# Two-layer streaming encoder on one core: raw weights, operand loads and tile choice in the seven-product MLP

## The chip, the cores and the metric

The kernel runs on one core of one Trainium2 chip. The metric is the device time of one execution in microseconds (us). The core has five engines, each with a queue of its own: TensorE (PE; its weight loads are PEld), VectorE (DVE), ScalarE (ACT), GpSimd (POOL) and SyncE (SP). In this kernel all the large transfers are issued from SP's queue.

## The reference

One step of an encoder with two trunk layers over 1024 prompt tokens and 32 sample tokens (1056 columns in all, model width 1024). Layer 0 mixes with an mLSTM, layer 1 with banded attention; each is followed by a layer norm and an MLP, which is all that matters here:

```python
        x = layer_norm(ALPHA * x + (1 + g1) * y, p['ln_g'][l, 0], p['ln_b'][l, 0])
        u = x * (1 + sc2) + sh2
        f = jnp.square(jax.nn.relu(u @ p['w_up'][l])) @ p['w_down'][l]
        x = layer_norm(ALPHA * x + (1 + g2) * f, p['ln_g'][l, 1], p['ln_b'][l, 1])
```

`w_up` is 1024 x 4096, `w_down` 4096 x 1024, all in float32.

## The kernel before

Every float32 operand is split into a high and a low part (`split`: a cast on ScalarE at L89, a subtraction on VectorE at L90), and a product is three matmuls (high x high, high x low, low x high).

The MLP of layer 1 is `mlp7`. The 1056 columns are cut into four quarters of `QN` = 264, and two quarters make a pair `tp` (`L.pairs` = 1, 0). Where it can, a 2 x 2 block product is made from seven block products instead of eight (`PRODS`, products 0 to 6); these use sums and differences of blocks, called forms.

**Up part.** 16 blocks `pb` of 256 columns of `w_up`. Ten (6 to 15) are first made plainly for pair 1 (`up_tile`, `up_unit`'s work, L1341 to L1376), while `tforms` makes the forms of `u` in `TF`, `ext` and `exu`. Then come 22 jobs (block, pair), numbered `j`; the last ones are blocks 11, 14, 12, 15, 13 for pair 0. A job is a `Seven`, whose `product(i)` is twelve matmuls (L1300). The jobs overlap: products are ordered by `7 * j + 2 * i`, so that a job's later products alternate with the next job's first. Product 6 ends with `h_forms`: it squares `H` (three buffers), splits it into `HL` and `HM` (one buffer each) and stores them, for blocks below 14 as the seven operand forms to `hd` in DRAM (L1172, L1177), for blocks 14 and 15 plainly to `hpl` (L1167).

**Weights.** `forms` is a generator for one block's weights: its first step issues two raw loads (L1248, tiles `rdn_u`, `rdn_d`, from a ring of three raw tiles), the later ones make the split forms `wf_u`, `wf_d`. `prep(n)` takes the first step, `advance(n, i)` the others, called after product `i` of block `n`.

**Down part.** 20 units: five groups `g` of blocks (`GRP`: two blocks in group 0, three in the others, so `kg` = 2 or 3), and in each four units `m` of 256 output columns. A unit is the seven products over both pairs (L1406), with an addition into `ACX` behind each (L986). `ACX` lies over the tiles of `TF`, and `L.reload(m)` (L1932) brings a quarter of it back from DRAM. The operands of a group are 14 loads (`fill`, `Rooms.load`, L1117) from `hd` into rooms: a list of quarter tiles, each with `KG` = 4 rooms, in `ep` (4), the two `u2` tiles (16 each), four `f4` tiles (16, over the place of `H`, `HL` and `HM`) and a ring tile (4). A load takes `kg` rooms from the head of the list, in one transfer for each run of adjacent ones. A group's rooms come back one form at a time during its last unit. The loads of group 0 begin in the up part, ten of them, as far as there are rooms.

**End.** Blocks 14 and 15 are made plainly from `hs`, four tiles in the place of the four `f4` tiles, loaded from `hpl` (L1472), with the columns in four blocks, and each block is normed and stored.

The order on each engine's queue is not that of the text. The text gives the order of importance; a planner that reckons with its own times for every instruction fixes the order at build time, except on PE, where in the marked regions (`manual_schedule`) the order of the text holds within the region. SP issues its transfers in the planned order, and each waits there until its tile is free or its data is ready.

Of the kernel before, what the change touches and what calls it, by code (L numbers as in the profile page):

```python
# [75 lines left out]
def trunk_kernel(ctx: ExitStack, tc: tile.TileContext, a, o):  # L76
# [10 lines left out]
    def split(dst_h, dst_l, src, eng=None):  # L87

        nc.scalar.copy(dst_h, src)  # L89
        (eng or nc.vector).tensor_sub(dst_l, src, dst_h.bitcast(F32))  # L90
# [1001 lines left out]
    GRP = [(0, 2), (2, 3), (5, 3), (8, 3), (11, 3)]  # L1092
# [31 lines left out]
    def mlp7(L):  # L1124
# [15 lines left out]
        rooms = Rooms()  # L1140

        def up_w(pb):
            if pb not in wups:
                wups[pb] = up_weights(l, pb)
            return wups[pb]
# [6 lines left out]
        def h_tile(pb, tp):  # L1152
            return hhp.tile([P, 6, QN], F32, tag="H", name=f"H{l}_{pb}_{tp}", bufs=3)

        def h_place(pb, tp):
            g = [i for i, (p0, kg) in enumerate(GRP) if p0 <= pb][-1]
            return hd[g][tp][:, :, pb - GRP[g][0]].rearrange("f p l t -> p f (l t)")

        def h_forms(pb, tp, H):

            nc.scalar.activation(H[:, 0:4], H[:, 0:4], AF.Square)
            hl = hhp.tile([P, 4, 2, QN], F32R, tag="HL", name=f"HL{l}_{pb}_{tp}", bufs=1)
            if pb >= NW:
                split(hl[:, :, 0], hl[:, :, 1], H[:, 0:4])
                for f, q, i in ((0, 1, 0), (0, 0, 1), (1, 1, 2), (1, 0, 3)):
                    t0 = (2 * tp + q) * QN
                    nc.sync.dma_start(hpl[2 * (pb - NW) + f, :, :, t0:t0 + QN], hl[:, i].bitcast(F32))  # L1167
                return
            dst = h_place(pb, tp)
            nc.vector.tensor_sub(H[:, 4:6], H[:, 0:3:2], bass.AP(H.tensor, H[:, 1].offset, [H.ap[0], [-QN, 2], [1, QN]]))  # L1170
            split(hl[:, :, 0], hl[:, :, 1], H[:, 1:5])
            nc.sync.dma_start(dst[:, 0:4], hl.bitcast(F32).rearrange("p f l t -> p f (l t)"))  # L1172
            nc.vector.tensor_sub(H[:, 1], H[:, 2], H[:, 4])
            nc.vector.tensor_sub(H[:, 3], H[:, 3], H[:, 1])
            hm = hhp.tile([P, 3, 2, QN], F32R, tag="HM", name=f"HM{l}_{pb}_{tp}", bufs=1)
            split(hm[:, :, 0], hm[:, :, 1], H[:, 1:6:2])
            nc.sync.dma_start(dst[:, 4:7], hm.bitcast(F32).rearrange("p f l t -> p f (l t)"))  # L1177

        def up_tile(pb, f, q):

            tp = q // 2
            ps = up_mm(pb, f, q)
            if (pb, tp) not in hts:
                hts[pb, tp] = [h_tile(pb, tp), 0]
            H = hts[pb, tp][0]
            nc.scalar.activation(H[:, ((1, 0), (3, 2))[f][q % 2]], ps, AF.Relu)
            hts[pb, tp][1] += 1
            if hts[pb, tp][1] == 4:
                h_forms(pb, tp, hts.pop((pb, tp))[0])
            flow.tick(QN / 96)  # L1190
# [42 lines left out]
        def moving(f, tp, hl, k):  # L1233
            if f in (B11, B21, B22, T4):
                kap, q = {B11: (0, 0), B21: (1, 0), B22: (1, 1), T4: (0, 1)}[f]
                return L.u4(hl, tp, kap, q)[:, k]
            if f == T3:
                return exts[tp][:, hl, k]
            return TF[tp, int(f == T2)][hl][:, k]
# [43 lines left out]
        class Seven:  # L1283
# [2 lines left out]
            def __init__(self, pb, tp, ws):  # L1286
                self.pb, self.tp, self.ws, self.ps = pb, tp, ws, {}

            def product(self, i):
                w, f, b, _, _ = PRODS[i]  # L1290
                pb, tp = self.pb, self.tp
                if i == 0:
                    self.H = h_tile(pb, tp)
                first = b not in self.ps
                if first:
                    self.ps[b] = mm(f"up{l}_{pb}_{tp}_{b}")[:, :QN]
                p, H = self.ps[b], self.H
                for k in range(4):
                    for n_, (wl, xl) in enumerate(((0, 0), (0, 1), (1, 0))):
                        nc.tensor.matmul(p, self.ws[w][:, wl, k], moving(f, tp, xl, k), start=first and k + n_ == 0,  # L1300
                                         stop=k == 3 and n_ == 2, skip_group_check=not first)
                if i in (0, 2, 3):
                    nc.scalar.copy(H[:, {0: 4, 2: 5, 3: 2}[i]], p)
                elif i in (1, 4, 5):
                    o_, x = {1: (1, 4), 4: (2, 2), 5: (0, 5)}[i]
                    nc.vector.tensor_add(H[:, o_], p, H[:, x])
                    if i == 5:
                        nc.scalar.activation(H[:, 0:3], H[:, 0:3], AF.Relu)
                else:
                    nc.scalar.activation(H[:, 3], p, AF.Relu)  # L1310
                    h_forms(pb, tp, H)
                flow.tick(QN / 64)

        tp0, tp1 = L.pairs
# [10 lines left out]
        jobs = [(n, tp) for n, (pb, tps) in enumerate(seq) for tp in tps]  # L1325
# [3 lines left out]
        def prep(n):  # L1329
            if n < len(makers):  # L1330
                preps[n] = makers[n]()
                next(preps[n])

        def advance(n, i):

            if n + 1 in preps and i in (0, 1, 3, 5):
                got[n + 1] = next(preps[n + 1])
            if i == 3:
                prep(n + 2)
        TF = {}  # L1340
        for i in range(2):  # L1341
# [12 lines left out]
        for j, pb in enumerate(rest):  # L1354
            for f in range(2):
                for q in L.quarters[:2]:
                    up_tile(pb, f, q)
                if (j, f) == (0, 1):
                    L.ready(2)
                    for n, tp in enumerate(L.pairs):  # L1360
                        for i, t in enumerate(L.scratch(n)):
                            TF[tp, i] = t
                    exts[tp1] = ring.tile([P, 2, KG, QN], F32R, tag="wc", name=f"exu_{l}", bufs=6)
                    tfs = [tf, tforms(tp1, exts[tp1])]
                at = 2 * j + f - 2 * len(rest) + 14
                if at == 11:
                    prep(0)
                for n in {1: (1,), 2: (1,), 3: (1,), 4: (1,), 5: (1,), 6: (1,), 7: (0,), 8: (0,), 11: (0, 2),
                          12: (2,), 13: (2, 0)}.get(at, ()):
                    if n < 2:  # L1370
                        next(tfs[n], None)
                    else:
                        got[0] = next(preps[0])
            del wups[pb]
            if j + 2 < len(rest):
                up_w(rest[j + 2])  # L1376
        fx, nfx, f4s = {}, {}, []
# [3 lines left out]
        def fill(g, into, most=99):  # L1381

            kg = GRP[g][1]
            if g >= len(GRP) - 2:
                rooms.free.sort(key=lambda r: any(r[0] is t for t in f4s) == (g == len(GRP) - 1))
            while want and len(rooms.free) >= kg and most:
                most -= 1
                tp, f = want.pop(0)
                into[tp, f] = rooms.load(hd[g][tp][f], kg)

# [23 lines left out]

        prep(1)
        got[0] = next(preps[0])
        lone = max(j for j, (_, tp) in enumerate(jobs) if tp == tp0)
        sevens = {}
        with tc.manual_schedule(engines={mybir.EngineType.PE}):
            for _, j, i in sorted((7 * j + 2 * i, j, i) for j in range(len(jobs)) for i in range(7)):  # L1420
                n, tp = jobs[j]
                if i == 0:
                    sevens[j] = Seven(seq[n][0], tp, got[n])
                sevens[j].product(i)
                if tp == seq[n][1][-1]:
                    advance(n, i)
                if j == lone and i == 6:
                    rooms.add(ep.tile([P, KG, 2, QN], F32R, tag="e", name=f"fx_e{l}"))
                    for t in L.rooms(tp0):
                        rooms.add(t)  # L1430
                if j > lone + 1:
                    if i in (0, 2, 4):
                        fill(0, fx, 1)
                    elif i == 6 and j < lone + 4:
                        L.reload(j - lone - 2)
        L.reload(2)
        nu = len(seq)
        hh_cm.__exit__(None, None, None)
        f4_cm = tc.tile_pool(name=f"f4{l}", bufs=1, reuse_waits="tile")
        f4p = f4_cm.__enter__()  # L1440
        f4s += [f4p.tile([P, KG, 2, QN], F32R, tag=f"f4{i}", name=f"fx_4{i}_{l}") for i in range(4)]
        for t in f4s:
            rooms.add(t)
        for t in L.rooms(tp1):
            rooms.add(t)
        fill(0, fx)
        with tc.manual_schedule(engines={mybir.EngineType.PE}):
            for i, (g, m, phases) in enumerate(units):
# [16 lines left out]
                if m == 3:  # L1465
                    assert not want
                    fx, nfx = nfx, {}
# [70 lines left out]
    for gi, grp in enumerate(((0, 1, 2), (3,))):  # L1538
        ws = {pr: [wblock(f"q{pr}_{half}", wq, 512 * half, 256 * pr) for half in range(2)] for pr in grp}
        for ti, (t0, n) in enumerate(TBS):  # L1540
# [7 lines left out]
            for fc in [f for pr in grp for f in (2 * pr, 2 * pr + 1)]:  # L1548
                g, r = fc // 2, 2 * (fc % 2)
# [309 lines left out]
    for ti in rev:  # L1859
        t0, n = TBS[ti]  # L1860
# [138 lines left out]
```

## Time and profile before

| what | value |
|---|---|
| median of 3 runs | 2477.54 us (2477.21 to 2479.55) |
| the profiled execution | 2478.93 us |
| its span in the profile | 2477.2 us |
| mean granted PE clock | 0.986 |
| instructions | 42903 |
| bytes moved by DMA | 335.17 MB |
| jobs of the up part on PE (L1300) | 1855 to 2094 us |
| down part on PE (L1406) | 2088 to 2400 us |
| last plain part (`hs`) on PE | 2406 to 2440 us |

Times in the profile are from the start of the span. A line such as `2104.11 12.06 SPq L1117 ... x12` means: from 2104.11 us on, for 12.06 us, twelve instructions of line 1117 on SP's queue; the brackets behind a line give how long the engine stood idle before it and what ended that. A line of the list of waits gives who waited for whom, the total in us, how often, and the longest.

### The profile page before, as it was taken

What the parts mean: (1) busy time and instruction counts of PE and PEld (TensorE: products, weight loads), DVE (VectorE), ACT (ScalarE), POOL (GpSimd) and SP (SyncE); (2) the same over time, 40 slices, a digit from 0 to 9 for tenths busy, and PEclk for the clock granted to TensorE, in tenths of its full rate; (3) what the DMA queues carried; (4) which work ended last, traced back from release to release, by engine and by line L of the source; (5) the groups of instructions that cost most, each with busy time, mean ns of one, the idle gap of its engine ahead of it and who ended that gap; (6) DMA issues with size and microseconds to landing.
All of it is one profiled execution on the core that took longest, in us unless ns stands there. A gap on an engine that the chain in (4) does not pass through costs nothing.

```text
span 2477.2 us, 42903 instructions
## 1 busy us (share of the span) xinstructions
PE 2391.2 (97%) x16580; PEld 2300.1 (93%) x16580; DVE 1921.3 (78%) x4340; ACT 1090.5 (44%) x2264; POOL 167.9 (7%) x315
## 2 busy tenths in 40 slices
PE   7999999999999999999999999999999997899997
PEld 4999999999999999999999877899999997899997
DVE  4898999778678679676597667747998887777768
ACT  4644456382211211212266567744866775222212
POOL 0211100000000000000001144400000000000003
PEclk9999999999999999999999999999999998999999
DMA  8433223313224224224132310052576788856632
GB/s 297 122 110 101 81 89 122 115 35 119 77 91 137 81 87 139 76 91 142 44 101 81 92 36 2 18 147 63 191 263 214 256 299 309 319 205 234 238 117 71
DMA packets 251072, 335.17 MB, mean 135 GB/s; under 512 B 12776, under 2 KB 201596, under 8 KB 249844
## 3 DMA queue, kind: packets, MB, share of 16 engines
q1 hardware_dynamic: 250868, 332.42, 41.0%
q8 instruction: 131, 2.15, 0.3%
q14 instruction: 73, 0.60, 0.1%
HBM read 255.50 MB, written 79.24 MB: 135 GB/s over the span
## 4 chain that ended last, share of the span: by engine, by line
PE 79%; DVE 10%; ACT 2%; DMA 2%; issue 2%; POOL 0%; SPq 0%; DVEq 0%; ACTq 0%; POOLq 0%
PE dn L1406 11%; PE up L1300 8%; PE up L120 6%; PE up L118 6%; PE up L119 6%; PE dn L119 5%; PE dn L118 5%; PE dn L120 5%; PE pv L1739 3%; PE s L1682 2%; PE pt L1717 2%; PE op_a L118 1%; PE op_a L119 1%; PE op_a L120 1%; PE o L118 1%
## 5 line engine op out<-in xcount | busy, mean ns | idle before, releaser
L1406 PE MATMUL dn<-fx,wf_d 128*128 128x264 f32 x2016 | 254.9, 286 | 17.0 <-DMA fx<-hd 12.0
L1406 PEld LDWEIGHTS dn<-fx,wf_d 128*128 128x128 f32 x2016 | 250.0, 189 | 18.5 <-DMA fx<-hd 12.2
L119 PE MATMUL dn<-h,w_dn 128*128 128x384 f32 (+1 forms) x768 | 249.5, 325 | 0.0
L118 PE MATMUL up<-U,w_up 128*128 128x384 f32 (+1 forms) x768 | 249.2, 325 | 0.0
L119 PE MATMUL up<-U,w_up 128*128 128x384 f32 (+1 forms) x768 | 247.9, 323 | 0.0
L118 PE MATMUL dn<-h,w_dn 128*128 128x384 f32 (+1 forms) x768 | 247.8, 323 | 0.0
L120 PE MATMUL up<-U,w_up 128*128 128x384 f32 (+1 forms) x768 | 247.6, 322 | 0.0
L120 PE MATMUL dn<-h,w_dn 128*128 128x384 f32 (+1 forms) x768 | 247.3, 322 | 0.0
L986 DVE SCALAR_TENSOR_TENSOR ACX<-dn,ada,ACX 128x264 f32<-128x264 f32 (+5 forms) x400 | 160.1, 427 | 66.7 <-PE dn L1406 47.5
L238 DVE SCALAR_TENSOR_TENSOR aacc<-rada,cs,aacc 128x256 f32<-128x256 f32 x448 | 190.4, 478 | 0.0
L986 DVE SCALAR_TENSOR_TENSOR acc<-dn,ada,acc 128x384 f32<-128x384 f32 (+2 forms) x256 | 119.4, 487 | 47.7 <-PE dn L120 46.4
L1025 ACT ACTIVATE r<-up 128x384 f32<-128x384 f32 (+1 forms) x96 | 44.3, 463 | 243.9 <-PE up L120 236.5
L1300 PE MATMUL up<-u,wf_u 128*128 128x264 f32 x1056 | 140.9, 286 | 8.5 <-ACT wf_u L89 8.0
L119 PEld LDWEIGHTS dn<-h,w_dn 128*128 128x128 f32 x768 | 144.5, 188 | 0.2 <-DVE h L1028 0.2
L120 PEld LDWEIGHTS dn<-h,w_dn 128*128 128x128 f32 x768 | 144.5, 188 | 0.0
L120 PEld LDWEIGHTS up<-U,w_up 128*128 128x128 f32 x768 | 144.3, 188 | 0.0
L118 PEld LDWEIGHTS up<-U,w_up 128*128 128x128 f32 x768 | 144.2, 188 | 0.1
L119 PEld LDWEIGHTS up<-U,w_up 128*128 128x128 f32 x768 | 144.2, 188 | 0.0
L118 PEld LDWEIGHTS dn<-h,w_dn 128*128 128x128 f32 x768 | 143.9, 187 | 0.2
L1300 PEld LDWEIGHTS up<-u,wf_u 128*128 128x128 f32 x1056 | 133.8, 189 | 9.3 <-ACT wf_u L89 8.2
L1027 DVE TENSOR_TENSOR r<-r 128x384 f32<-128x384 f32 (+1 forms) x96 | 50.0, 523 | 102.2 <-ACT h L1026 101.8
L89 ACT CAST w_up<-raw_up 128x1024 fp32r<-128x1024 f32 x52 | 54.3, 1047 | 140.3 <-DMA raw_up<-in_w_up_dram 122.6
(386 smaller groups left out, 6581.5 us busy)
## 6 DMA issues: line engine op xcount, KB each, us to landing
rada<-in_w_ada_dram SPq DMA_DIRECT2D x64, 512.0 KB
hd<-HL SPq DMA_DIRECT2D x28, 1056.0 KB
raw_up<-in_w_up_dram SPq DMA_DIRECT2D x52, 512.0 KB
fx<-hd SPq DMA_DIRECT2D x46, 528.0 KB
hd<-HM SPq DMA_DIRECT2D x28, 792.0 KB
raw_dn<-in_w_down_dram SPq DMA_DIRECT2D x36, 512.0 KB
ada_room<-in_w_ada_dram SPq DMA_DIRECT2D x32, 512.0 KB
rdn_u<-in_w_up_dram SPq DMA_DIRECT2D x32, 512.0 KB
```

The source lines that it names most:

```text
L89: nc.scalar.copy(dst_h, src)
L118: nc.tensor.matmul(ps, wh, mov(0, k), start=(k == 0), stop=False)
L119: nc.tensor.matmul(ps, wh, mov(1, k), start=False, stop=False)
L120: nc.tensor.matmul(ps, wl, mov(0, k), start=False, stop=(k == nk - 1))
L238: nc.vector.scalar_tensor_tensor(acc[:, cnd], raw[:, k], sc, acc[:, cnd], op0=ALU.mult, op1=ALU.add)
L986: nc.vector.scalar_tensor_tensor(xs, ps[:, off + o:off + o + mm_], gate[:, fc, cnd:cnd + 1], xs, op0=ALU.mult, op1=ALU.add)
L1027: nc.vector.tensor_mul(r, r, r)
L1300: nc.tensor.matmul(p, self.ws[w][:, wl, k], moving(f, tp, xl, k), start=first and k + n_ == 0, stop=k == 3 and n_ == 2, skip_group_check=n ...
L1406: nc.tensor.matmul(p, ws[w][:, wl, k], t[:, s0, xl], start=first and k + n_ == 0, stop=k == kg - 1 and n_ == 2, skip_group_check=not first)
L1682: nc.tensor.matmul(s[:, b, :w], qst, kk[i][:, g, k0 + j0:k0 + j0 + w], start=(i == 0), stop=(i == 1))
L1717: nc.tensor.transpose(pt[:kp, j - j0, pr * P:(pr + 1) * P], ps_[pr][:, j * P:j * P + kp], ident)
L1739: nc.tensor.matmul(pv[64 * e:64 * e + 64, :nq], V[:kp, vt0 + j, g * 64:(g + 1) * 64], pts[e][:kp, j, :nq], start=(j == 0), stop=(j == nt - 1))
```

## The change

- `prep(n + 2)`, which issues the raw weight loads of the block after the next, is called after product 2 instead of product 3, in the up jobs and in the down units.
- A function `up_end` is called in the last up job's product 6, after its ReLU and before its `h_forms`. It issues `L.reload(2)`, adds the rooms over `u2` of the second pair, and fills the rest of group 0. Before, these stood behind the loop, and the `f4` rooms were added ahead of the `u2` ones.
- In the up jobs behind the lone one, the loads of group 0 are called after products 2, 4 and 6 instead of 0, 2 and 4, and the first two reloads after product 0 instead of 6.
- The steps of `tforms` move one place later in the plain up part: six for pair 0 to places 2 to 7 (from 1 to 6), two for pair 1 to places 8 and 9 (from 7 and 8).
- In `fill`, the list of rooms is sorted from group 2 on and at each load (before: from group 3 on and once per call). Three of the four `f4` tiles count. They are preferred for group 2 and for the last four loads of group 3, and come last for the first ten of group 3 and for group 4.

```diff
-            def product(self, i):
+            def product(self, i, ended=None):
...
                     nc.scalar.activation(H[:, 3], p, AF.Relu)
+                    if ended:
+                        ended()
                     h_forms(pb, tp, H)
...
-            if i == 3:
+            if i == 2:
                 prep(n + 2)
...
-                for n in {1: (1,), 2: (1,), 3: (1,), 4: (1,), 5: (1,), 6: (1,), 7: (0,), 8: (0,), 11: (0, 2),
+                for n in {2: (1,), 3: (1,), 4: (1,), 5: (1,), 6: (1,), 7: (1,), 8: (0,), 9: (0,), 11: (0, 2),
                           12: (2,), 13: (2, 0)}.get(at, ()):
...
-            if g >= len(GRP) - 2:
-                rooms.free.sort(key=lambda r: any(r[0] is t for t in f4s) == (g == len(GRP) - 1))
             while want and len(rooms.free) >= kg and most:
                 most -= 1
+                if g >= len(GRP) - 3:
+                    late = g == len(GRP) - 1 or g == len(GRP) - 2 and len(into) < 10
+                    rooms.free.sort(key=lambda r: any(r[0] is t for t in f4s[:3]) == late)
                 tp, f = want.pop(0)
                 into[tp, f] = rooms.load(hd[g][tp][f], kg)
...
+        def up_end():
+            L.reload(2)
+            for t in L.rooms(tp1):
+                rooms.add(t)
+            fill(0, fx)
...
-                sevens[j].product(i)
+                sevens[j].product(i, up_end if j == len(jobs) - 1 else None)
...
                 if j > lone + 1:
-                    if i in (0, 2, 4):
+                    if i in (2, 4, 6):
                         fill(0, fx, 1)
-                    elif i == 6 and j < lone + 4:
+                    if i == 0 and j < lone + 4:
                         L.reload(j - lone - 2)
-        L.reload(2)
...
         for t in f4s:
             rooms.add(t)
-        for t in L.rooms(tp1):
-            rooms.add(t)
         fill(0, fx)
```

## The prediction

> **What bounds the kernel now.** I read the page first: engine shares, then the chain.
>
> ```profile
> PE 2391.2 (97%) x16580; PEld 2300.1 (93%) x16580; DVE 1921.3 (78%) x4340; ACT 1090.5 (44%) x2264; POOL 167.9 (7%) x315
> ...
> PE 79%; DVE 10%; ACT 2%; DMA 2%; issue 2%; POOL 0%; SPq 0%; DVEq 0%; ACTq 0%; POOLq 0%
> ```
>
> TensorE (PE) is the bound almost everywhere; the change removes no matmul. It can only touch the few places where PE stands still, so the second view is the list of PE's waits from 1780 us on, the stretch that the edits reach (second layer's MLP).
>
> ```profile
> PE dn L1406 <- DMA fx<-hd: 12.0, 1, 12.0
> PE up L1300 <- ACT wf_u L89: 8.0, 1, 8.0
> PE dn L118 <- DMA hs<-hpl: 4.9, 1, 4.9
> PE dn L1406 <- DVE ACX L986: 3.7, 3, 1.6
> PE up L118 <- ACT w_up L89: 2.8, 2, 2.6
> ...
> PE up L120 <- DVE w_up L90: 1.9, 2, 1.2
> ```
>
> Three single waits make up 24.9 us. I call them A (8.0, weights for an up product), B (12.0, operands for the down part) and C (4.9, `hs`); the last two rows are D. Each also costs clock. The third view, stretches of 5 us, shows it (columns: PE, PEld, DVE, ACT, POOL busy with counts, then the granted clock, the DMA share and GB/s):
>
> ```profile
> 1790.00:1795.00 5.00, 2.62 (x14) 2.41 (x15) 5.00 (x7) 1.99 (x3) 0.00 (x0) 0.75 1.00 315
> 1795.00:1800.00 5.00, 5.00 (x27) 5.00 (x27) 4.97 (x6) 3.17 (x4) 0.00 (x0) 0.57 0.80 292
> ...
> 2075.00:2080.00 5.00, 5.00 (x26) 4.79 (x25) 4.78 (x9) 3.69 (x7) 0.00 (x0) 0.58 1.04 393
> 2080.00:2085.00 5.00, 5.00 (x43) 5.00 (x42) 2.65 (x6) 1.25 (x2) 0.00 (x0) 1.00 0.37 121
> ...
> 2405.00:2410.00 5.00, 4.19 (x17) 4.22 (x18) 0.00 (x0) 0.00 (x0) 0.00 (x0) 0.50 0.99 417
> ```
>
> After A, PE at a clock of 0.58 does 26 matmuls in 5 us where it does 43 at 1.00. PE's own rows, which the terms below use:
>
> ```profile
> 2064.81 1.63 PE L1300 MATMUL up<-TF,wf_u 128*128 128x264 f32 x12
> 2074.48 3.30 PE L1300 MATMUL up<-u,wf_u 128*128 128x264 f32 x12 [8.04 <-ACT wf_u L89]
> 2077.57 2.36 PE L1300 MATMUL up<-exu,wf_u 128*128 128x264 f32 x12
> ...
> 2092.87 1.61 PE L1300 MATMUL up<-u,wf_u 128*128 128x264 f32 x12
> ...
> 2100.21 1.00 PE L1406 MATMUL dn<-fx,wf_d 128*128 128x264 f32 x6 [0.68 <-DVE ACX L986]
> 2113.21 5.06 PE L1406 MATMUL dn<-fx,wf_d 128*128 128x264 f32 x24 [12.01 <-DMA fx<-hd]
> ```
>
> What holds A and B is SyncE's queue (SP), through which all these transfers are issued in one order:
>
> ```profile
> 2017.58 0.34 SPq L1117 DMA_DIRECT2D fx_e<-hd  x1
> ...
> 2056.69 1.89 SPq L1117 DMA_DIRECT2D fx<-hd  x2
> 2061.67 2.71 SPq L1167 DMA_DIRECT2D hpl<-HL  x4
> 2064.43 0.61 SPq L1932 DMA_DIRECT2D ACX<-xsp  x1
> 2065.09 1.45 SPq L1248 DMA_DIRECT2D rdn_u<-in_w_up_dram  x2
> ...
> 2095.77 0.47 SPq L1117 DMA_DIRECT2D fx<-hd  x1
> 2099.78 0.37 SPq L1172 DMA_DIRECT2D hd<-HL  x1
> 2103.17 0.36 SPq L1177 DMA_DIRECT2D hd<-HM  x1
> 2103.58 0.48 SPq L1248 DMA_DIRECT2D rdn_d<-in_w_down_dram  x1
> 2104.11 12.06 SPq L1117 DMA_DIRECT2D fx<-hd  x12
> ```
>
> The raw weights for which A waits are issued at 2065.09, behind four stores that wait for `HL`. The operands for which B waits are issued from 2104.11, behind the last block's two stores. The chain agrees and gives the landing times:
>
> ```profile
> 2065.09 8.70 DMA rdn_u<-in_w_up_dram
> ...
> 2105.17 8.00 DMA fx<-hd
> ```
>
> **A: raw weights one step earlier, reloads earlier, operand loads later.** `prep(n + 2)` moves from product 3 to product 2 of a block. Blocks interleave, and the previous block's last product, which calls `h_forms`, lies between the two; so the raw pair is asked for ahead of those stores. The reloads move from the end of a block to its start, the loads from products 0, 2, 4 to 2, 4, 6. The queue is full, so I price by bytes:
>
> ```profile
> 2000.00:2070.00 70.00, 66.04 (x541) 65.62 (x539) 58.47 (x99) 50.86 (x87) 0.00 (x0) 0.99 0.95 329
> ...
> fx<-hd SPq DMA_DIRECT2D x46, 528.0 KB
> ...
> hpl<-HL SPq DMA_DIRECT2D x16, 264.0 KB
> ```
>
> At 329 GB/s, a load of 528 KB (0.541 MB) takes 1.64 us, four stores of 264 KB 3.3 us. Before, eight loads (the first at 2017.58, the last two at 2056.69), both reloads and the four stores precede the late pair. After, the stores fall behind it, both reloads are still ahead, and by the new pattern only six loads are: 3.3 + 2 × 1.64 = 6.6 us less, and A shrinks from 8.0 to 1.4 us. The clock comes on top: the two groups of twelve behind A start 3.09 and 2.20 us apart (2074.48, 2077.57, and the next at about 2079.77 by the 2.36 us, less a pipelined 0.16) where twelve take 1.63 less 0.17 = 1.46: 1.63 + 0.74 = 2.4 us. A gives 6.6 + 2.4 = **9.0 us**. Bounds: 3.3 (only the stores pass) to 10.4 (all).
>
> The Trainium skill, in "TensorE: Matmul & The Clock Gate", Part 1, says that the clock is halved after an idle window of about 3.4 us and released after a busy one. Rows 1790 to 1800 speak partly against it: D's gaps are 2.6 and 1.2 us, none as long as that window, and yet the clock falls to 0.57. By the page a rest of 1.4 us keeps full speed and the 2.4 us are won, by the row it may not: 9.0 by the one, 6.6 by the other.
>
> **B: the last operands ahead of the last stores.** `up_end` runs between the last product's ReLU and `h_forms`. It issues `reload(2)`, adds the four tiles that lie over `u2[0]`, and fills the last four of the fourteen group-0 operands there; before, these four went into `f4` tiles, which lie over `H`, `HL` and `HM` and had to wait for them. The wait that takes its place: `u2[0]` is read by the very last up product, so SP stands until that is done, and block 15's stores and the next raw weights stand behind it.
> The last up product starts at 2092.87 and is over at about 2094.5; PE ran out of operands at 2101.2 (the end of the row at 2100.21), 6.7 us later. Issued 0.5 us after the product and landing as slowly as now (8.0 us), the first of the four comes at +8.5: 1.8 us late. The others follow at 1.64 us each while a product of six matmuls takes 0.73, three times 0.9: 4.5 us late in the end. So 12.0 becomes 4.5 at the slowest, 0 if the queue has drained (0.37 busy at 2080). I take 3.5, nearer the slow end because A's saving brings the last blocks closer together. The clock loss behind B now is 24 matmuls in 5.06 − 0.16 us against 24 × 0.122 = 2.9: 2.0 us; half of it stays. B gives 8.5 + 1.0 = **9.5 us**; bounds 3 and 14.
> Work that now hides in B's hole loses its cover: `h_forms` of the last block and the weight forms on VectorE (DVE).
>
> ```profile
> 2110.00 0.43 DVE L1264 TENSOR_TENSOR s_d<-rdn_d,rdn_d 128x256 f32<-128x256 f32 x1 [5.12 <-DMA rdn_d<-in_w_down_dram]
> ...
> 2110.00:2200.00 90.00, 83.12 (x660) 82.36 (x661) 73.13 (x183) 19.61 (x45) 0.00 (x0) 0.96 0.63 230
> ```
>
> DVE idles 5.1 us there and is then busy 73 of 90 us; PE already waits 3.7 us for its additions into `ACX`. Without the hole some of this grows. Between 0 and 5.1 I take **−3.5 us**, by the 3.7 row.
>
> **C: other tiles for `hs`.** `hs` lies in the four `f4` tiles. The list of free rooms, followed through the code load by load, gives this. Before, group 4 (the last) has its fifth and sixth form in part in `f4` 0 and its last in `f4` 1 and 2, read to the very end; `f4` 3 is free. The queue confirms it, one early and three late:
>
> ```profile
> 2346.99 0.44 SPq L1472 DMA_DIRECT2D hs<-hpl  x1
> ...
> 2398.78 2.44 SPq L1472 DMA_DIRECT2D hs<-hpl  x3
> ...
> 2405.81 0.58 PE L118 MATMUL dn<-hs,w_dn 128*128 128x288 f32 x1 [4.94 <-DMA hs<-hpl]
> ```
>
> After, the sort sends group 4 past `f4` 0 to 2 altogether; only its first two forms lie in `f4` 3, which is free ten products of nine matmuls (11 us) before the end. So three loads can go at about 2347 and the fourth lands in time; cuts of loads into pieces rise from 110 to 113 in all, nothing. The wait of 4.9 goes, and with it a clock of 0.50 for 17 matmuls at twice the time (17 × 0.12 = 2.0). Next late would be the weights, which are cast before then. C gives **6.5 us**; bounds 4 and 7.
>
> **D: `tforms` one step later.** It takes VectorE work (5.00 of 5.00 busy in the row at 1790) off the point where `w_up` is late. Of D, the 1.2 us on DVE can go; the 2.6 us wait for ScalarE's cast, which `tforms` does not feed there. With a share of the clock (27 matmuls instead of 43, 2.0 us) I take **+1.0 us**; bounds −2 (the same work delays later weights) and 3.
>
> **Sum.** 9.0 + 9.5 − 3.5 + 6.5 + 1.0 = 22.5 us. The profiled execution took 2478.9 us (span 2477.2 and 1.7 around it); it becomes 2456.4. It stands 1.4 us above the median of the runs, so the forecast is **2455.0 us**.
>
> **Rivals.**
> *The queue is full anyway.* Between 2000 and 2070 the DMA engines are busy 0.95 of the time; what passes the stores only makes other bytes late: A keeps its lower bound 3.3, B gives 3, C stays, D nothing, no growth on DVE: 12.8 us, 2464.7 us. For it: the share; against it: 0.37 at 2080 to 2085, and no store passed is needed by PE soon.
> *It does not do what it says.* The order of SP's queue is planned, not that of the text: `hs` 3 was issued 52 us ahead of 0 to 2. If the planner puts weights and operands behind the stores again, C alone remains: 2471.0 us.
> *SP is held, and the ups run late.* This ends slower. A raw pair needs its tile back from DVE's last split:
>
> ```profile
> SPq L1248 <- DVE wf_u L90: 45.9, 24, 2.2
> ```
>
> Asked 1.46 us earlier, SP would stand that much longer, and the stores of `HL` behind it. `HL` has one buffer, ScalarE's next cast into it waits for the landed store, and ScalarE's copies that free PE's accumulators stand behind that cast. It decides once a store is later than the spare part of a block's 7 × 1.46 = 10.2 us; then each of some 20 blocks loses up to 1.46: 29 us, against which C and half of B (11 us) stand: 2495 us. Against it: no PE wait of this kind among the rows, and three `H` buffers. The Trainium skill, in "DMA: Bandwidth & Descriptors", section on the anatomy of one DMA, says that a DMA's wait is made on the issuing sequencer. The SP wait above agrees.
>
> **How the numbers follow.** Forecast 0.63; full queue 0.16; not done 0.12; SP held 0.07; 0.02 for mishaps. Own bounds of the first: 2443 (22.5 and 12 more: A whole 1.4, B whole 4.5, DVE 3.5, others 2.5) to 2462 (A's clock not won, B 3.5 less, D nothing). The range 2443 to 2470 takes in the full queue and leaves out the rest, about 2 in 10. A measurement of this kernel can tell 0.2% (5 us) from no change. Faster: the first two and most of the third, 0.87; same 0.06; slower 0.07.
>
> **What would show it.** Right: the `rdn_u` pair ahead of the last `hpl` stores in SP's queue and A under 3 us; four `fx` loads between the last up product and the last `HL` store, B under 5; three `hs` loads near 2330 and no wait for `hs`; clock near 1.00 after each; a little more waiting for `ACX`. Wrong: a new wait of PE for `H` or for accumulators in the ups, or a wait of 10 us for `fx` at the start of the down part's second group.

## The result and the profile after

The changed kernel takes 2464.86 us (median of 4, 2464.21 to 2465.22), the kernel before 2478.55 (median of 4, 2477.21 to 2481.89): 13.7 us less, a ratio of 0.9942 [0.9925, 0.996]. Its profiled execution took 2464.7 us with a span of 2462.6, 14.6 us less than the 2477.2 of before. The forecast was 22.5 us less, so its sign held, the time lies in its range of 2443 to 2470 us, and 0.6 of its gain came.

The page after, engine shares and chain:

```profile
PE 2387.9 (97%) x16580; PEld 2296.7 (93%) x16580; DVE 1918.8 (78%) x4340; ACT 1089.9 (44%) x2264; POOL 167.3 (7%) x315
...
PE 76%; DVE 11%; DMA 4%; ACT 2%; issue 2%; POOL 1%; SPq 0%; DVEq 0%; ACTq 0%; POOLq 0%
```

TensorE's waits after 1780 us (total, count, longest):

```profile
PE dn L1409 <- DVE ACX L986: 14.0, 4, 11.3
PE dn L1409 <- DMA fx<-hd: 4.2, 2, 3.4
...
PE dn L1409 <- DVE wf_d L90: 1.7, 1, 1.7
PE up L120 <- DVE w_up L90: 1.6, 3, 0.9
PE up L1300 <- ACT wf_u L89: 0.6, 1, 0.6
```

A went from 8.0 to 0.6, B from 12.0 to 4.2, C and the 2.6 of D are gone. In their place there is one new wait, put down to `ACX` additions: 11.3 us long, where the three `ACX` waits of before made 3.7 in all. I call it E.

To see where the 14.6 us lie I cut the span at three rows: the first and last up product with `u`, and the first product with `hs`. Before, then after (ns of one, then from and to in us):

```profile
L1300 PE MATMUL up<-u,wf_u x1056: 278/284/589, 1855.2 to 2094.2; 128*128 128x264 f32 x176
L118 PE MATMUL dn<-hs,w_dn x128: 274/285/580, 2405.8 to 2462.6; 128*128 128x256 f32 x96, 128*128 128x288 f32 x32
```

```profile
L1300 PE MATMUL up<-u,wf_u x1056: 278/284/390, 1851.9 to 2079.2; 128*128 128x264 f32 x176
L118 PE MATMUL dn<-hs,w_dn x128: 274/285/368, 2393.2 to 2447.8; 128*128 128x256 f32 x96, 128*128 128x288 f32 x32
```

| part | before | after | difference |
|---|---|---|---|
| up to the first `u` product (D) | 1855.2 | 1851.9 | -3.3 |
| up part (A) | 239.0 | 227.3 | -11.7 |
| down part (B, and C's wait of 4.9) | 311.6 | 314.0 | +2.4 |
| `hs` products to the end (C's clock) | 71.4 | 69.4 | -2.0 |

The last row goes to the end of the span: the last `hs` product of before starts at 2462.6, later than the 2440 us of the table ahead of the prediction.

About 2 us of the up part's gain is only moved: before, 21 down matmuls lie among the last up products (12 from 2088.54 and 9 from 2091.78), after only 3 (from 2077.51), and 18 × 0.122 = 2.2. So A brought 11.7 − 2.2 = 9.5, C 4.9 + 2.0 = 6.9, D 3.3, and B with all that it set off **cost** 2.4 + 4.9 − 2.2 = 5.1 us. Forecast were 9.0, 6.5, 1.0, and for B a gain of 9.5 − 3.5 = 6.0. A and C came close, D brought 2.3 more than forecast, and B is off by 11.1 us.

SyncE's queue shows the edits at work, and what E is:

```profile
2053.74 2.67 SPq L1248 DMA_DIRECT2D rdn_u<-in_w_up_dram  x2
...
2057.37 2.71 SPq L1167 DMA_DIRECT2D hpl<-HL  x4
...
2083.65 2.44 SPq L1117 DMA_DIRECT2D fx<-hd  x4
2089.82 0.37 SPq L1172 DMA_DIRECT2D hd<-HL  x1
...
2097.04 13.54 SPq L1117 DMA_DIRECT2D fx<-hd  x12
2110.99 0.32 SPq L1117 DMA_DIRECT2D fx_w<-hd  x1
2112.92 2.97 SPq L1248 DMA_DIRECT2D rdn_d<-in_w_down_dram  x3
```

The `rdn_u` pair now stands ahead of the `hpl` stores, and the four `fx` loads of group 0 go 6 us before the last block's first `hd` store: as forecast. From 2097.04 the first loads of group 1 follow, nine operands in thirteen transfers. Their sizes (DMA issues from 2096 to 2112 us, KB each):

```profile
fx<-hd SPq DMA_DIRECT2D x4, 792.0 KB
fx<-hd SPq DMA_DIRECT2D x4, 528.0 KB
fx<-hd SPq DMA_DIRECT2D x4, 264.0 KB
fx_w<-hd SPq DMA_DIRECT2D x1, 792.0 KB
```

These are 7128 KB, 7.3 MB, and nobody needs them before the four units of group 0 are through. At 2112.92 the raw weights of unit 3, still in group 0, get their tile back from VectorE and are asked for behind all of it (units are numbered from 0). The chain, ScalarE's and VectorE's rows and then TensorE's follow the delay:

```profile
2112.92 10.60 DMA rdn_d<-in_w_down_dram
```

```profile
2123.62 0.41 ACT L89 CAST wf_d<-rdn_d 128x256 fp32r<-128x256 f32 x1 [12.60 <-DMA rdn_d<-in_w_down_dram]
```

```profile
2112.22 1.68 DVE L986 SCALAR_TENSOR_TENSOR ACX<-dn,ada,ACX 128x264 f32<-128x264 f32 x4
2124.06 0.43 DVE L90 TENSOR_TENSOR wf_d<-rdn_d,wf_d 128x256 fp32r<-128x256 f32 x1 [10.16 <-ACT wf_d L89]
...
2126.75 1.94 DVE L986 SCALAR_TENSOR_TENSOR ACX<-dn,ada,ACX 128x232 f32<-128x232 f32 x6
```

```profile
2091.00 3.07 PE L1409 MATMUL dn<-fx,wf_d 128*128 128x264 f32 x12 [3.40 <-DMA fx<-hd]
2094.84 3.02 PE L1409 MATMUL dn<-fx,wf_d 128*128 128x264 f32 x12 [0.77 <-DMA fx<-hd]
...
2127.51 6.83 PE L1409 MATMUL dn<-fx,wf_d 128*128 128x264 f32 x36 [11.29 <-DVE ACX L986]
```

The weights take 10.60 us to land. ScalarE stands 12.60 for them, VectorE's weight split 10.16 for ScalarE, and the `ACX` additions stand behind that split in VectorE's order. No accumulator comes free, and TensorE stands. The row of the waits names VectorE, which had been idle for 10.16 us, up to 2124.06; only the last 3.4 us of TensorE's 11.29 are VectorE's own work, on the weight forms and the first additions. The releaser named is the last link of a chain that began at a transfer. The windows show that stretch and the clock behind it (columns as in the prediction):

```profile
2090.00:2095.00 5.00, 3.14 (x13) 2.58 (x14) 3.76 (x9) 1.26 (x2) 0.00 (x0) 0.65 1.02 362
2095.00:2100.00 5.00, 5.00 (x29) 5.00 (x30) 1.86 (x4) 0.00 (x0) 0.00 (x0) 0.67 1.05 404
...
2115.00:2120.00 5.00, 1.22 (x11) 1.01 (x9) 0.00 (x0) 0.00 (x0) 0.00 (x0) 0.88 1.01 407
...
2125.00:2130.00 5.00, 2.49 (x11) 2.52 (x12) 4.88 (x16) 1.45 (x4) 0.00 (x0) 0.50 0.26 83
2130.00:2135.00 5.00, 5.00 (x34) 5.00 (x33) 2.93 (x7) 0.98 (x3) 0.00 (x0) 0.76 0.01 3
```

From 2115 to 2120 TensorE is busy for 1.22 us, VectorE and ScalarE not at all, and the DMA engines are full. 10.60 us at 390 GB/s, the mean over that time, are 4.1 MB, over half of those 7.3 MB: raw weights of 256 and 384 KB landed behind megabytes that nobody was waiting for. The Trainium skill, in "DMA: Bandwidth & Descriptors", section on queues, rings and completion order, says that on each DMA engine descriptors are consumed in ring order. The landing time agrees.

### The profile page after: what moved, and what is told of

Its sections match the earlier page's. It is cut to its first block, busy times and chain, and to the rows that moved or that the text cites. A ratio compares the mean times of both kernels' runs of the same rounds, so it can differ in the third digit from the quotient of the medians.

```text
span 2462.6 us, 42910 instructions
## 1 busy us (share of the span) xinstructions
PE 2387.9 (97%) x16580; PEld 2296.7 (93%) x16580; DVE 1918.8 (78%) x4340; ACT 1089.9 (44%) x2264; POOL 167.3 (7%) x315
## 4 chain that ended last, share of the span: by engine, by line
PE 76%; DVE 11%; DMA 4%; ACT 2%; issue 2%; POOL 1%; SPq 0%; DVEq 0%; ACTq 0%; POOLq 0%
PE dn L1409 11%; PE up L1300 9%; PE up L118 5%; PE dn L119 5%; PE dn L118 5%; PE up L120 5%; PE up L119 5%; PE dn L120 5%; PE pv L1744 3%; PE s L1687 2%; PE pt L1722 2%; PE o L118 1%; PE o L119 1%; PE o L120 1%; PE op_b L118 1%
```

## The experiments

After the result my theory was: A and C work as forecast, and E comes from the order in a full queue, because filling hole B takes away the time in which the queue drained ahead of the raw weights. The rival was the forecast's own reason for a loss: VectorE's work, now without cover. The first four kernels separate the edits and move the suspected loads. Ratios, with a 95% interval, are to runs of the kernel before taken beside them: 2480.85 us for the first four kernels, 2480.3 for the last four.

**The sort alone** (before, with the new order of rooms in `fill`):

```diff
-            if g >= len(GRP) - 2:
-                rooms.free.sort(key=lambda r: any(r[0] is t for t in f4s) == (g == len(GRP) - 1))
             while want and len(rooms.free) >= kg and most:
                 most -= 1
+                if g >= len(GRP) - 3:
+                    late = g == len(GRP) - 1 or g == len(GRP) - 2 and len(into) < 10
+                    rooms.free.sort(key=lambda r: any(r[0] is t for t in f4s[:3]) == late)
```

> The kernel before with the new sort of rooms alone. Every theory: the wait for hs (4.9 us) and its half clock (2.0 us) go and nothing else does: 6 to 7 us faster, ratio 0.9972 to 0.9976. If the wait for hs goes and the time does not follow, part C of the prediction was mis-sized.

2479.38 us, 0.9991 [0.998, 1.0001]: nothing measurable, where 6 to 7 us were expected. The wait for `hs` shrank from 4.9 to 2.0 but is not gone, and two loads are still issued late:

```profile
PE dn L118 <- DMA hs<-hpl: 2.0, 2, 1.8
```

```profile
2350.93 0.91 SPq L1473 DMA_DIRECT2D hs<-hpl  x2
2401.59 0.34 SPq L1473 DMA_DIRECT2D hs<-hpl  x1
2404.91 0.42 SPq L1473 DMA_DIRECT2D hs<-hpl  x1
```

So the sort alone lets two loads go early where one did before, and the wait stays in part.

**Raw weights early, alone** (before, with one line changed):

```diff
-            if i == 3:
+            if i == 2:
                 prep(n + 2)
```

> The kernel before with prep(n + 2) after product 2 alone. Additive theory (the prediction's): A goes, B stays 12 us: 7 to 9 us faster, ratio 0.9965 to 0.9972. Full queue theory (a saved wait comes back at the next place that needs the same queue): A under 2 us, B grows from 12 to 18 or more, no more than 3 us faster, ratio 0.9988 to 1.000.

2477.45 us, 0.9977 [0.9967, 0.9987]. The up part runs from 1857.0 to 2087.7, 230.7 us, 8.3 shorter than before, and A is down to 0.6 in the waits; 1.1 of the 8.3 is nine down matmuls that moved out of the part (12 among the last up products instead of 21). Most of it is given back in the down part (318.7 against 311.6):

```profile
PE dn L1406 <- DMA fx<-hd: 14.5, 1, 14.5
PE dn L1406 <- DVE ACX L986: 5.5, 3, 2.8
```

B grew by 2.5 and the `ACX` waits by 1.8. Counted from the first `u` product, TensorE stands ready for B's operands at 240.5 us instead of 246.0, and they come at 255.0 instead of 258.0: 5.5 us sooner for the one, 3.0 for the other. Part of a saved wait is waited again at the next place that hangs on the queue. The 3.4 us that are left lie between what the additive and the full-queue theory expected.

**`up_end` alone** (before, with the last four group-0 loads between the last ReLU and `h_forms`, and the order of rooms that comes with it):

```diff
-            def product(self, i):
+            def product(self, i, ended=None):
...
+                    if ended:
+                        ended()
                     h_forms(pb, tp, H)
...
+        def up_end():
+            L.reload(2)
+            for t in L.rooms(tp1):
+                rooms.add(t)
+            fill(0, fx)
...
-        L.reload(2)
...
-        for t in L.rooms(tp1):
-            rooms.add(t)
```

> The kernel before with up_end and its rooms alone. Additive theory: A stays 8 us, B under 5 us, no new wait: 9 to 11 us faster, ratio 0.9956 to 0.9964. Full queue theory: A stays, B under 3 us since the queue drains during A, but in unit 2 or 3 of group 0 a new wait of 4 to 9 us for the raw weights that stand behind group 1's loads: 3 to 8 us faster, ratio 0.997 to 0.9988.

2476.23 us, 0.9984 [0.9974, 0.9993], 4.6 us less. A stays, B is gone, and E is there in full, with none of the other edits:

```profile
PE dn L1408 <- DVE ACX L986: 16.0, 4, 11.6
PE up L1300 <- ACT wf_u L89: 7.1, 1, 7.1
```

So E is the price of `up_end`, and about as large as the wait it removes. The wait for `hs` is gone too, without the new sort. The down part is 309.2 us, 2.4 less than before; as C's 4.9 are gone from it, the rest of it is 2.5 longer.

**Group 1's loads behind the next raw weights** (after; the first loads of group 1 are called after product 2 of unit 1, when the raw weights of unit 3 have been asked for):

```diff
-                if m == (2 if g else 1) and more:
+                if m == 2 and g and more:
                     fill(g + 1, nfx)
...
-                unit(g, m, phases, got[nu + i], lambda j: advance(nu + i, j), after)
+                def step(j, i=i, m=m, g=g):
+                    advance(nu + i, j)
+                    if not g and m == 1 and j == 2:
+                        fill(1, nfx)
+                unit(g, m, phases, got[nu + i], step, after)
```

> The changed kernel, with group 1's first loads called after product 2 of unit 1 (behind the raw weights of unit 3) instead of before the unit. Full queue theory: the wait of 11.3 us in unit 2 shrinks to under 4 us and the down part's second group starts without a long wait: 2453 to 2458 us, ratio 0.990 to 0.992. VectorE theory (forms and additions of group 0 are what limits there): the wait stays about 11 us wherever the raw weights stand: 2463 to 2467 us. Raw tile theory (the second raw tile of unit 3 is free only once unit 2's forms are made, so that SP stands and group 1's loads behind it are late): the 11.3 us go, 5 to 10 us come at the start of group 1: 2460 to 2466 us.

2457.61 us, 0.9903 [0.9887, 0.9919]: E is gone from its place, and the down part is 306.3 us instead of 314.0. But a smaller wait stands one unit later, inside unit 3, at ScalarE's cast of the raw weights of unit 4, which now stand behind the same loads:

```profile
PE dn L1409 <- ACT wf_d L89: 7.2, 1, 7.2
```

```profile
2106.39 0.38 SPq L1248 DMA_DIRECT2D rdn_d<-in_w_down_dram  x1
2106.82 6.17 SPq L1117 DMA_DIRECT2D fx<-hd  x10
...
2115.35 2.35 SPq L1248 DMA_DIRECT2D rdn_d<-in_w_down_dram  x2
```

By the VectorE rival, moving loads could not have brought anything. The third theory on record, that SP stands for a raw tile and group 1's loads behind it come late, had 2460 to 2466 us and a wait at the start of group 1. SP did stand 9.6 us for a raw tile, but no wait for group 1's operands came. The queue theory holds for E; it had not seen that the next pair would stand behind the same loads.

The next four kernels follow from that: spread the loads over two gaps, and take back each of the other edits singly.

**The loads split** (after; four of group 1's loads behind unit 3's raw weights, then `reload(3)`, the rest behind unit 4's):

```diff
                 if i == 0:
-                    L.reload(3)
-                if i == 0:
...
-                if m == (2 if g else 1) and more:
+                if m == 2 and g and more:
                     fill(g + 1, nfx)
...
+                def step(j, i=i, m=m, g=g):
+                    advance(nu + i, j)
+                    if not g and j == 2 and m in (1, 2):
+                        fill(1, nfx, 4 if m == 1 else 99)
+                        if m == 1:
+                            L.reload(3)
+                unit(g, m, phases, got[nu + i], step, after)
```

> The changed kernel with group 1's first loads in two parts: four behind the raw weights of unit 3, the other five behind those of unit 4, and the last reload of ACX behind the first four. Theory that the order in the full queue decides: both the 11.3 us of the changed kernel and the 7.2 us that the run with all loads behind unit 3's weights had at the start of unit 4 go, no PE wait over 4 us between the groups; ratio to before 0.986 to 0.989. Theory that the bytes alone decide (whatever comes last is late): 6 to 8 us of waiting for fx come back in units 4 and 5, ratio 0.990 to 0.992.

2452.41 us, 0.9882 [0.9868, 0.9896]: faster than both kernels, 27.9 us below the 2480.3 of before beside it. No wait of TensorE for `ACX` or for the weights is left that is longer than 1.6:

```profile
PE dn L1409 <- DMA fx<-hd: 4.3, 1, 4.3
PE dn L1409 <- DVE ACX L986: 3.7, 4, 1.6
...
PE dn L1409 <- ACT wf_d L89: 1.7, 2, 1.0
```

```profile
2115.00:2120.00 5.00, 4.70 (x39) 4.52 (x38) 4.73 (x16) 1.52 (x4) 0.00 (x0) 1.00 1.02 387
```

The same stretch, a DMA share of 1.02 where it was 1.01, and four engines at work: the queue is as full as in the changed kernel, only the order in it differs. The 6 to 8 us of waiting for `fx` in units 4 and 5, which the theory that the bytes alone decide expected, did not come. The down part is 302.2 us. Without C (311.6 − 4.9) and with the 2.2 that moved in, before's would be 308.9; so B is worth 6.7 us here, near the 6.0 forecast for it. Whether another order on VectorE, with the additions ahead of the weight split, would have hidden E as well, no run tests.

**The old sort** (after, with the sort lines of before):

> The changed kernel with the old sort of rooms. By the list of rooms, group 4 then has its second pair of forms in f4 2 and 3 and nothing in f4 0 and 1, all four free 11 us before the end, so the sort is not what freed hs: no wait for hs, the time of the changed kernel, ratio to before 0.993 to 0.9955. If the new sort is what freed them, 5 to 7 us slower, ratio 0.996 to 0.998.

2464.24 us, 0.9931 [0.9919, 0.9944], the same as with the new sort within the intervals. No wait for `hs`. With the first experiment: the new sort does nothing here that the time shows, alone or with the rest. It is `up_end` that frees the tiles: it puts the rooms over `u2` ahead of the `f4` rooms, and by the list of rooms, followed through the code once more, group 4 then has only its second pair of forms in `f4`, instead of operands that are read to the very end.

**The old places of `tforms`** (after, with the table of before):

```diff
-                for n in {2: (1,), 3: (1,), 4: (1,), 5: (1,), 6: (1,), 7: (1,), 8: (0,), 9: (0,), 11: (0, 2),
+                for n in {1: (1,), 2: (1,), 3: (1,), 4: (1,), 5: (1,), 6: (1,), 7: (0,), 8: (0,), 11: (0, 2),
```

> The changed kernel with tforms at its old places. If the later tforms is what took away D: PE's waits for w_up come back to 4 to 5 us around 1790 with a clock near 0.6, 4 to 6 us slower than the changed kernel, ratio to before 0.996 to 0.997. If the prediction's size (1.0 us) was right: ratio 0.994 to 0.995.

2469.22 us, 0.9952 [0.994, 0.9965]: 5.0 us more than the old-sort kernel beside it (2464.24), which has the new table. By its ratio alone it lies between the two sizes expected; the 5.0 us side by side speak for the larger. The waits of before are back, those for ScalarE's cast too, and so is the lower clock. The wait and a window of this kernel, then the same window of the changed one:

```profile
PE up L118 <- ACT w_up L89: 2.8, 2, 2.6
```

```profile
1795.00:1800.00 5.00, 3.08 (x16) 2.87 (x17) 5.00 (x8) 1.53 (x2) 0.00 (x0) 0.69 1.00 312
```

```profile
1795.00:1800.00 5.00, 5.00 (x43) 5.00 (x42) 5.00 (x7) 3.11 (x6) 0.00 (x0) 1.00 0.71 231
```

Across all kernels, the first product with `u` starts at 1855.2 to 1859.6 (mean 1857.8) in the five profiles with the old table, and at 1849.9 to 1853.8 (mean 1851.8) in the five with the new one: 6.0 us.

**Raw weights late again** (after, with `prep(n + 2)` at product 3):

> The changed kernel with prep(n + 2) back at product 3. Order in the queue: without the early raw weights A comes back only in part, since the reloads and loads are already moved: 2 to 8 us; the wait in unit 2 (11.3) shrinks by as much, because the queue drains in A. Total within 4 us of the changed kernel, ratio to before 0.993 to 0.997. Additive theory (the prediction's 9.0 for A): 7 to 10 us slower, ratio 0.997 to 0.9985.

2473.47 us, 0.9964 [0.995, 0.9978], 9.2 us more than the old-sort kernel beside it. The up part is 240.0 us, nothing gained, and both waits stand side by side:

```profile
PE dn L1409 <- DVE ACX L986: 15.0, 3, 11.6
PE up L1300 <- ACT wf_u L89: 6.8, 1, 6.8
```

So A hangs on that one line: the new pattern of reloads and loads brings nothing by itself. With the line moved, the whole change has an up part 3.4 us shorter than that line alone (227.3 against 230.7), of which 1.1 is nine more down matmuls that moved out. The 9.2 us fit the 9.0 forecast for A. My queue theory had E shrink here, since the up part ends later. It did not: 11.6 as in `up_end` alone. Group 1's loads are called at unit 1 of group 0, so they move with the end of the up part, and the raw weights stand behind them wherever that falls.

## Why the prediction was right, and where it was not

**A** was right in mechanism and edit: wait 0.6 where 1.4 was forecast, the clock near 1.00 behind it, 9.5 us for 9.0.

**B, the wait itself** was right: 4.2 left where 3.5 was forecast, and `u2[0]` holds SP no longer than reckoned. Of its clock term the opposite came: behind the shorter waits of 3.40 and 0.77 the clock is at 0.65 and 0.67 for 10 us, and 13 and 29 matmuls ran where about 27 and 43 fit: 28 × 0.116 = 3.2 us lost, where half of 2.0 was to stay. This part of B, half a clock loss won, failed too: 2.2 us.

**The −3.5 us for work that loses its cover in hole B is the step that failed**, in mechanism and in size. I had VectorE's additions grow by what it idled in the hole, "between 0 and 5.1". The `ACX` waits grew by 10.3 (14.0 less 3.7) and the clock behind them cost about 2 more (45 matmuls from 2127.5 to 2135 where 64 fit, 19 × 0.116), and for 7.8 us of its longest, 2116.2 to 2124.06, VectorE was idle. What had used the hole was the queue: while TensorE stood, SP went on issuing loads and the DMA engines moved them, and the raw weights of unit 3 were asked for soon after TensorE had begun unit 1. The start of unit 1 (a unit is 84 matmuls) and the issue of those weights, before and then after:

```profile
2118.11 0.89 PE L1406 MATMUL dn<-fx_e,wf_d 128*128 128x264 f32 x6
2122.45 9.34 SPq L1248 DMA_DIRECT2D rdn_d<-in_w_down_dram  x3
```

```profile
2097.67 1.18 PE L1409 MATMUL dn<-fx_e,wf_d 128*128 128x264 f32 x6
```

That is 4.3 us after the start of unit 1 before, and 15.2 us after it (2112.92) with the change. I listed the engines that work in the hole and not the transfers, although this window of before would have shown it, all engines idle and the DMA engines full:

```profile
2105.00:2110.00 5.00, 0.00 (x0) 0.00 (x0) 0.00 (x0) 0.00 (x0) 0.00 (x0) 0.50 1.02 343
```

Of the 11.1 us that B is off, about 9.0 lie in this step, 2.2 in the clock term and 0.7 in the wait; 0.9 less of waiting for the weight forms stands against them.

**C** had the right size, 6.9 for 6.5, from the wrong edit: I gave it to the sort, and it is `up_end`'s order of rooms.

**D** was mis-sized: 1.0 forecast, 3.3 in this pair of profiles, 5.0 between two kernels side by side and 6.0 over ten profiles, above my bound of 3. The failed step is "the 2.6 us wait for ScalarE's cast, which `tforms` does not feed there": in the changed kernel that wait goes too, and with both gaps gone the clock stays at 1.00. It does not always go: with the old sort and with the raw weights late again, both with the new table, a wait for ScalarE's cast of 1.6 and of 2.25 us is left, and behind the second the clock is at 0.68. Which link joins that wait to `tforms` (a raw tile freed by VectorE, or the order of the casts) I have not shown.

**The rivals.** "The queue is full anyway" gave 2464.7 us, and the time came out there, by chance: its terms were 3.3 for A, 3.0 for B, 6.5 for C and nothing for D, and measured were 9.5, −5.1, 6.9 and 3.3. Its mechanism is E's, but not in its places: A won in full, and the bytes that were late were the raw weights of the down part. There was luck in the range too: the forecast's own bounds ended at 2462, and the range reached to 2470 for this rival's sake. "It does not do what it says" fell with the queue's order. "SP is held" did not show: no row of TensorE's waits in the up part is above 0.9 after the change. The last sentence of my list of signs, a wait of 10 us at the start of the second group, named the right loads and the wrong victim: they were not late themselves, they made others late.

## What to carry to other kernels

Filling the hole behind a wait on a full queue did not remove the wait here, but handed it to what stood next in the order: for each hole that a change closes, list the transfers that drained in it as well as the engines that worked in it. Prefetches for a later stage belong behind the small loads that the next step needs; here that order alone, with the same loads, was worth 12 us (2464.86 to 2452.41). And follow a wait back past the engine that its row names: here VectorE was named, and the cause lay in a transfer two engines back.

## What the runs showed of the hardware

Small loads behind a full queue took 10.60 us to land, and nothing in the row of their issue shows it. The DMA engines moved 404 and 407 GB/s in the windows around E, where I had priced them at 329.

Waits shorter than expected halve the clock, and not always the same ones. Two gaps of 2.6 and 1.2 us gave 0.69 with the old `tforms`, and 3.40 and 0.77 us gave 0.65; the 1.7 us wait for `wf_d` was followed by full speed (1.00). With the raw weights late again, a single gap of 2.25 us (TensorE's row at 1805.36) was followed by 0.68, and gaps of 1.17 and 2.30 us (rows at 2100.83 and 2104.88 of the same kernel) by 1.00. The Trainium skill, in "TensorE: Matmul & The Clock Gate", Part 1, asks for an idle window of about 3.4 us. The second pair fits it; the first and the single gap of 2.25 us do not. What decides between them no run here shows; that short gaps add up does not explain it, since 1.17 and 2.30 us kept the full clock.
